# The second half of an embedding gate: seven block products for three pairs of K tiles, and low parts made by accumulating transfers

## The chip, the cores and the metric

The kernel runs on one core of one Trainium2 chip. Its time is the device time of one execution in microseconds, taken as the median of several runs. A profile of one execution gives the start and length of every instruction on the engines: TensorE (PE; its weight loads are PEld), VectorE (DVE), ScalarE (ACT), GpSimd (POOL) and SyncE (SP), whose queue issues most of the DMAs.

## What is computed

One layer of a decoder block on 256 tokens of width 2048, all in fp32. The change touches only the last step:

```
x = layer_norm(ALPHA * x + ffn, ln2_g, ln2_b)
x = x + jax.nn.sigmoid(x @ w_ple_gate) * (p @ w_ple_proj)   # w_ple_gate: 2048 x 2048
```

Before it come a combined input projection, gated linear attention and forgetting attention, their merge and output projection, a layer norm, a gated MLP with a causal convolution and another layer norm.

## The kernel before

**Weights in two parts.** TensorE multiplies in a rounded format. Each fp32 weight w is therefore split into hi, a rounded copy, and lo = w - hi, and activations likewise. A product of K tiles is three matmuls: hi by hi, hi by lo and lo by hi.

**Units.** All weights stream through the chip as 284 units, each of two K tiles (128 rows each) by 1024 columns, in two halves (one K tile each) of 512 KB. `prep()` (L207) makes a unit ready: for each half a load `raw` on SP's queue (L216), the rounded copy `hi` on ScalarE (`copy`, L112) and the subtraction `lo` on VectorE (L220). The tiles come from rings: 5 `raw`, 6 `hi`, 6 `lo`. A tile of a ring can be written again when the last reader of the tile six (five) places earlier is done. `unit()` prepares three units ahead. `prep_s()` (L167) makes a unit ready for seven products instead of eight: it takes four differences of weight blocks on VectorE (`differences`, L146) and splits the result into four hi and four lo pieces (b11 of 512 columns, b2, t13 and t24 of 1024). Each earlier stage that uses it has its list of pairs (`GV_S`, `WO_S`, `DN_S` and others); the gate has none.

**The gate.** It runs in two halves, pg0 (units 268 to 275, output columns 0 to 1023) and pg1 (units 276 to 283). `x_half` (L347) accumulates one half: four PSUM banks, one for each of two token tiles by two blocks of 512 columns; `x_mm` (L320) issues the matmuls, 24 of 512 columns per unit (2 K tiles, 2 token tiles, 3 products, 2 blocks). The units run one after the other, but the last two of pg1 (`tail=2`) run block by block, so that the first blocks are complete earlier. With `fine=True` (pg1 only) block (1,1) lies in two banks of 256 columns, `pg` and `pg_11b`, for all eight units; its matmuls there have 256 columns, twice as many.

**The end of a block.** `ev_o` (L1450 on) makes the output from a complete bank: tanh on ScalarE (L1459, `tho`), two VectorE operations (L1460 `tho`, L1462 `res`) that apply it to the projection of p (`ppk`) and add the layer's z, and a store on SP (L1464). pg0's four stores are held back and issued by `store_first` after pg1's first unit.

**Order.** The instructions of SP stay in written order. Those of the other engines are ordered ahead of time by a planner, and each engine's queue is in order: an instruction that waits holds back what stands behind it. POOL does little: some small operations, and DMAs of intermediate sums (`sd`, `td`) to DRAM in earlier stages.

Of the kernel before, what the change touches and what calls it, by code (L numbers as in the profile page):

```python
# [9 lines left out]
F32 = mybir.dt.float32  # L10
F32R = mybir.dt.float32r
BF16 = mybir.dt.bfloat16
U8 = mybir.dt.uint8
AF = mybir.ActivationFunctionType
ALU = mybir.AluOpType
# [4 lines left out]
P = 128  # L20
D = 2048
S = 256
# [26 lines left out]
OUT_ORDER = (tuple(range(8)), (0, 1, 3, 2, 5, 4, 6, 7))  # L49
# [3 lines left out]
WO_S = ((1, 3, 5), (1, 3, 5))  # L53
WO_C = (0, 2, 4, 6, 7)

DN_ORDER = (tuple(range(NF // 2)),
            (0, 1, 2, 3, 5, 4, 7, 9, 6, 11, 8, 13, 10, 15, 12, 17, 14, 16, 18, 19, 20, 21))
DN_S = ((1, 3, 5, 7, 9, 11, 13, 15, 17, 19), (1, 3, 5, 7, 9, 11, 13, 15, 17))


WO_T = ((3, 5), (1, 3, 5))
DN_T = ((3, 9, 15, 19), (5, 9, 13, 17))
AFF1 = ((0, 2, 3), (0, 2))
AFF2 = ((0, 2), (0, 2))
LN_ORDER = (1, 0, 3, 2)
# [7 lines left out]
def tile_block(ctx: ExitStack, tc: tile.TileContext, wu, wfv, wpp, xT_in, x_in, pT_in, wlr,  # L73
               chan, gnorm, lng, ident_in, mask_in, cmask_in, out):
    nc = tc.nc
# [26 lines left out]
    def t2(name):  # L102
        return sm.tile([P, 512], F32, tag="t2", bufs=6, name=name)
# [17 lines left out]
    for _ in range(8):  # L121
# [4 lines left out]
    NU = wu.shape[0]  # L126
    dn0 = NU - 16 - NF
    s_units = {b + nh * len(order[nh]) + i
               for b, order, sset in ((52, WO_ORDER, GV_S), (68, WO_ORDER, GR_S),
                                      (120, OUT_ORDER, WO_S), (dn0, DN_ORDER, DN_S))  # L130
               for nh in range(2) for i, n in enumerate(order[nh]) if n in sset[nh]}
    ready = {}

# [8 lines left out]
    def lo_tile(u, name):  # L142
        o = 0 if any(u in r for r in UA) else LO_SHIFT
        return rlo.tile([P, 1152], F32R, tag="lo", name=f"lo{name}")[:, o:o + 1024]
# [62 lines left out]
    def prep(pinned=False):  # L207
        u = n_prep[0]
        n_prep[0] += 1
        if u in s_units:  # L210
            prep_s(u)
            return
        his, los = [], []
        for h in range(2):
            raw = ring.tile([P, 1024], F32, tag="raw", bufs=5, name=f"raw{u}_{h}")
            nc.sync.dma_start(raw, wu[u, :, h * 1024:(h + 1) * 1024])  # L216
            hi = rhi.tile([P, 1024], F32R, tag="hi", name=f"hi{u}_{h}")
            copy(hi, raw)
            lo = lo_tile(u, f"{u}_{h}")
            i = nc.vector.tensor_tensor(lo, raw, hi.bitcast(F32), ALU.subtract)  # L220
            if pinned:
                tc.keep_in_program_order(i)
            his.append(hi)
            los.append(lo)
        ready[u] = (his, los)
# [212 lines left out]
    for u in range(8):  # L438
        hi, lo = fvu[u]
        for j in range(2):  # L440
            kt = 2 * u + j
            a = xT[kt // 4][:, kt % 4, :]
# [6 lines left out]
            for t, i, c in seq:  # L449
                o, n = fch[c]  # L450
                w, x = prods[t][i]
                nc.tensor.matmul(fbk[t][c][:, 0:n], lhsT=x, rhs=w[:, o:o + n],  # L452
                                 start=kt == 0 and i == 0, stop=kt == 15 and i == 2)
# [32 lines left out]
    for t in range(2):  # L486
        for c, (o, n) in enumerate(fch):
            n = min(n, 1024 - o)
# [279 lines left out]
        return o  # L768

    def s_half(nm, nh, order, sset, cl, st, zof, ev, tail=0, mid={}, end=None, ahead=3,  # L770
               residual=True):

        if nh == 0:
            C = [[mmtile(f"{nm}0_{t}{c}") for c in range(2)] for t in range(2)]
            p1, p5 = [mmtile(f"{nm}0_p{i}") for i in (1, 5)]
            p6, p7 = [mxtile(f"{nm}0_p{i}") for i in (6, 7)]
        else:  # L780
            C = [[f(f"{nm}1_{t}{c}") for c in range(2)] for t, f in enumerate((mxtile, mmtile))]
            p1, p5, p6, p7 = [mmtile(f"{nm}1_p{i}") for i in (1, 5, 6, 7)]
        prods = (p1, C[0][0], C[0][1], p5, p7, p6, C[1][0])
        left = (0, 1, 6, 3, 5, 4, 2)
        n, ns = len(order), len(sset)
        todo = {id(C[t][c]): 6 * (n - ns) for t in range(2) for c in range(2)}
        for p in prods:
            todo[id(p)] = todo.get(id(p), 0) + 3 * ns
        total = dict(todo)

        def mm(ps, x, w):
            nc.tensor.matmul(ps, lhsT=x, rhs=w, start=todo[id(ps)] == total[id(ps)],  # L792
                             stop=todo[id(ps)] == 1)
            todo[id(ps)] -= 1

        def classic(pair, w, toks=(0, 1), cs=(0, 1)):
            for j in range(2):
                for t in toks:
                    ah, al = cl(pair, j, t)
                    for x, v in ((ah, w[0][j]), (ah, w[1][j]), (al, w[0][j])):  # L800
                        for c in cs:
                            mm(C[t][c], x, v[:, c * 512:c * 512 + 512])

        def strassen(pair, ops):
            for ps, i, (hi, lo) in zip(prods, left, ops):
                ah, al = st(pair, i)
                for x, v in ((ah, hi), (ah, lo), (al, hi)):
                    mm(ps, x, v)

        def fold():  # L810
            g0, g1 = 2 * nh, 2 * nh + 1
            u = t2("fold")
            axpy = lambda z, p: nc.vector.scalar_tensor_tensor(z, z, ALPHA, p, ALU.mult, ALU.add)
            add = lambda z, p: nc.vector.tensor_tensor(z, z, p, ALU.add)
            if not residual:
                copy(zof(0, g0), p1)
                for o, x, p in ((u, zof(0, g0), p6), (zof(0, g1), u, p5), (zof(1, g0), u, p7),
                                (zof(1, g1), zof(1, g0), p5)):
                    nc.vector.tensor_tensor(o, x, p, ALU.add)
                return  # L820
            copy(u, p1)
            axpy(zof(0, g0), p1)
            add(u, p6)
            axpy(zof(0, g1), u)
            add(zof(0, g1), p5)
            add(u, p7)
            axpy(zof(1, g0), u)
            add(u, p5)
            axpy(zof(1, g1), u)

        for i, pair in enumerate(order[:n - tail]):
            (strassen if pair in sset else classic)(pair, unit())
            if i in mid:
                mid[i]()
            if pair in sset and not set(order[i + 1:]) & set(sset):
                fold()
        us = [unit(ahead) for _ in range(tail)]

        def tail_mm(t, c, i):
            classic(order[n - tail + i], us[i], (t,), (c,))  # L840
            if i == tail - 1:
                ev(t, c, C[t][c])

        if tail:
            end(tail_mm)
            return
        for t in range(2):
            for c in range(2):
                ev(t, c, C[t][c])
# [599 lines left out]
        for store in stores:  # L1449
            store()  # L1450

    for nh in range(2):
        def ev_o(t, c, ps, ab=(0, 512), nh=nh):
            th = t2("tho")
            r = t2("res")
            e = slice(*ab)
            w = slice(c * 512 + ab[0], c * 512 + ab[1])
            o = slice(nh * 1024 + w.start, nh * 1024 + w.stop)
            nc.scalar.activation(th[:, e], ps, AF.Tanh, bias=0.0, scale=0.5)  # L1459
            nc.vector.scalar_tensor_tensor(th[:, e], th[:, e], 1.0, pp[nh][:, t, w],  # L1460
                                           ALU.add, ALU.mult)
            nc.vector.scalar_tensor_tensor(r[:, e], th[:, e], 0.5, z2[nh][:, t, w],  # L1462
                                           ALU.mult, ALU.add)
            store = lambda: nc.sync.dma_start(out[t, :, o], r[:, e])  # L1464
            if nh == 0:
                stores.append(store)
            else:
                store()
        x_half(f"pg{nh}", x2T, 16, ev_o, pulls=2, begin=begin2 if nh == 0 else None,
               tail=2 if nh == 1 else 0, mid=((mid3, 4), (store_first, 0))[nh],  # L1470
               fine=nh == 1)
    assert n_used[0] == NU, (n_used[0], NU)


# [9 lines left out]
def _xst(w):  # L1484

    k, n = w.shape
    a = w.reshape(k // 256, 2, P, n // 1024, 1024).transpose(3, 0, 2, 1, 4)
    return a.reshape((k // 256) * (n // 1024), P, 2048)


def _sst(w, orders, ssets):


    out = []
    for nh, (order, sset) in enumerate(zip(orders, ssets)):
        for n in order:
            b = [[w[(2 * n + j) * P:(2 * n + j + 1) * P,
                    nh * 1024 + c * 512:nh * 1024 + c * 512 + 512] for c in range(2)]
                 for j in range(2)]
            out.append(np.concatenate([b[0][1], b[0][0], b[1][1], b[1][0]] if n in sset  # L1500
                                      else b[0] + b[1], 1))
    return np.stack(out)
# [11 lines left out]
def _layout(i):  # L1514
# [4 lines left out]
    for n in range(16):  # L1519
        br.append(bg[n:n + 1])  # L1520
        if n % 2 == 0:
# [6 lines left out]
         _sst(c("gv", 2048), WO_ORDER, GV_S), _sst(c("gr", 2048), WO_ORDER, GR_S), m[PSM1:]] + br  # L1528
        + [_sst(i["w_out"][0], OUT_ORDER, WO_S), gu,
           _sst(i["w_down"][0], DN_ORDER, DN_S),  # L1530
           _xst(i["w_ple_gate"][0])], 0)
    wfv = np.concatenate([c("fv", 1024), c("glr", 16), c("ff", 8)], 1)
    wfv = wfv.reshape(8, 2, P, NS).transpose(0, 2, 1, 3)
    x = _fold(i["x"][0])
# [40 lines left out]
```

## Time and profile before

| what | us |
|---|---|
| median of 3 runs | 1662.37 (1661.83 to 1663.08) |
| span of the profiled execution | 1661.1 |
| PE busy | 1655.3 |
| DVE busy | 1278.4 |
| ACT busy | 887.5 |
| POOL busy | 61.3 |
| DMA, mean | 231 GB/s |

The page gives no time of its own for the profiled execution beside its span; the median of the runs is 1.3 us above that span. The busy times are sums over the whole span. Times in the views count from the span's start; the gate's second half lies between some 1612 and 1657 us.

### The profile page before, as it was taken

How to read it: one execution, taken by the hardware profiler on the slowest of the kernel's cores; microseconds unless marked ns; L12 is line 12 of the kernel's file. 1: busy time of each engine (PE TensorE's matmuls, PEld its weight loads, DVE VectorE, ACT ScalarE, POOL GpSimd, SP SyncE). 2: the span in 40 equal slices, each digit the busy share in tenths (PEclk: the TensorE clock that was granted, in tenths of full speed). 3: DMA queues.
4: the chain of work that ended last, by engine and by line, in shares of the span. 5: the costliest groups of instructions: out<-in, count | busy, mean ns of one | idle time of the engine just before them, and what ended most of it. 6: DMA issues, size and time to landing. Idle time of an engine off the chain costs nothing.

```text
span 1661.1 us, 24309 instructions
## 1 busy us (share of the span) xinstructions
PE 1655.3 (100%) x8935; PEld 1438.3 (87%) x8935; DVE 1278.4 (77%) x1927; ACT 887.5 (53%) x1297; POOL 61.3 (4%) x204
## 2 busy tenths in 40 slices
PE   9999999999999999999999999999999999999999
PEld 9988888888888888888898888888888888888887
DVE  7666877888876757888987777877777787898774
ACT  6655555555554654455575455555555555556543
POOL 0100000000000000000010010000000000000000
PEclk9999999999999999999999999999999999999999
DMA  8745455546564557878856587777777668798554
GB/s 321 251 164 172 169 176 171 188 158 199 196 232 172 174 181 275 309 244 301 315 171 206 207 291 266 251 243 249 254 249 255 204 226 322 275 364 316 178 188 158
DMA packets 101959, 383.74 MB, mean 231 GB/s; under 512 B 11544, under 2 KB 12832, under 8 KB 95696
## 3 DMA queue, kind: packets, MB, share of 16 engines
q1 hardware_dynamic: 97584, 359.11, 62.1%
q0 software_dynamic: 4256, 23.08, 3.7%
q8 instruction: 70, 1.15, 0.3%
q14 instruction: 49, 0.40, 0.1%
HBM read 358.02 MB, written 24.13 MB: 230 GB/s over the span
## 4 chain that ended last, share of the span: by engine, by line
PE 98%; DMA 0%; DVE 0%; ACT 0%; POOL 0%; SPq 0%; issue 0%; POOLq 0%
PE dn L792 11%; PE psu L287 9%; PE psg L287 9%; PE psm L287 7%; PE pg L333 5%; PE psu L289 5%; PE psg L289 5%; PE gv L792 4%; PE wo L792 4%; PE psm L289 4%; PE psa L287 4%; PE dn_p L792 3%; PE gr L333 3%; PE fv L452 2%; PE gr L792 2%; PE psa L289 2%
## 5 line engine op out<-in xcount | busy, mean ns | idle before, releaser
L220 DVE TENSOR_TENSOR lo<-raw,hi 128x1024 fp32r<-128x1024 f32 x502 | 611.0, 1223 | 240.4 <-ACT hi L112 238.7
L112 ACT ACTIVATE hi<-raw 128x1024 fp32r<-128x1024 f32 x502 | 528.4, 1058 | 430.5 <-issue 169.2
L287 PE MATMUL psu<-x1T,hi 128*128 128x512 f32 x688 | 240.4, 392 | 0.0
L287 PE MATMUL psg<-x1T,hi 128*128 128x512 f32 x672 | 234.8, 392 | 0.0
L289 PE MATMUL psu<-x1T,lo 128*128 128x256 f32 x688 | 192.4, 280 | 0.0
L289 PE MATMUL psg<-x1T,lo 128*128 128x256 f32 x672 | 187.9, 280 | 0.0
L287 PE MATMUL psm<-xT,hi 128*128 128x512 f32 x512 | 181.2, 396 | 0.0
L287 PEld LDWEIGHTS psu<-x1T,hi 128*128 128x128 f32 x688 | 129.2, 188 | 27.6
L287 PEld LDWEIGHTS psg<-x1T,hi 128*128 128x128 f32 x672 | 126.2, 188 | 26.9
L289 PE MATMUL psm<-xT,lo 128*128 128x256 f32 x512 | 143.2, 280 | 0.0
L289 PEld LDWEIGHTS psu<-x1T,lo 128*128 128x128 f32 x688 | 130.7, 190 | 0.0
L289 PEld LDWEIGHTS psg<-x1T,lo 128*128 128x128 f32 x672 | 127.6, 190 | 0.0
L287 PEld LDWEIGHTS psm<-xT,hi 128*128 128x128 f32 x512 | 96.2, 188 | 19.7
L792 PE MATMUL dn<-hi,hC 128*128 128x512 f32 x400 | 111.3, 389 | 0.0
L289 PEld LDWEIGHTS psm<-xT,lo 128*128 128x128 f32 x512 | 97.2, 190 | 0.1
L287 PE MATMUL psa<-oT,hi 128*128 128x512 f32 x256 | 89.5, 392 | 0.0
L792 PEld LDWEIGHTS dn<-hi,hC 128*128 128x128 f32 x400 | 75.0, 188 | 15.6
L112 ACT ACTIVATE hi_t<-raw 128x1024 fp32r<-128x1024 f32 x40 | 42.5, 1063 | 66.0 <-DVE raw L148 51.5
L112 ACT ACTIVATE hi_b<-raw 128x512 fp32r<-128x512 f32 x66 | 55.4, 842 | 40.9 <-DMA raw<-in_wu_dram 15.2
L289 PE MATMUL psa<-oT,lo 128*128 128x256 f32 x256 | 71.6, 280 | 0.0
L194 DVE TENSOR_TENSOR lo_b<-raw,hi_b 128x512 fp32r<-128x512 f32 x66 | 62.5, 954 | 9.9 <-ACT hi_b L112 9.9
L333 PE MATMUL pg<-hi,x2T 128*128 128x512 f32 (+1 forms) x256 | 69.7, 380 | 0.0
(372 smaller groups left out, 3126.3 us busy)
## 6 DMA issues: line engine op xcount, KB each, us to landing
raw<-in_wu_dram SPq DMA_DIRECT2D x555, 512.0 KB, 4.9
td<-in_wu_dram SPq DMA_DIRECT2D x13, 1024.0 KB, 8.4
td<-td POOLq DMA_DIRECT2D x13, 1024.0 KB, 6.9
td<-td SPq DMA_DIRECT2D x13, 1024.0 KB, 7.5
hS<-sd SPq DMA_DIRECT2D x19, 512.0 KB, 7.6
fvraw<-in_wfv_dram SPq DMA_DIRECT2D x13, 524.0 KB, 6.9
sd<-hs POOLq DMA_DIRECT2D x20, 256.0 KB, 5.4
lnb<-in_lng_dram SPq DMA_DIRECT2D x4, 1024.0 KB, 9.8
```

Of the source, the lines that this page charges most:

```text
L112: return nc.scalar.activation(o, i, AF.Copy, bias=0.0, scale=scale)
L194: nc.vector.tensor_tensor(lo, src, hi.bitcast(F32), ALU.subtract)
L220: i = nc.vector.tensor_tensor(lo, raw, hi.bitcast(F32), ALU.subtract)
L287: nc.tensor.matmul(ps, lhsT=hi[i // 8 if hoff == 0 else 0][:, w0 % 1024:w0 % 1024 + P], rhs=a[:, kt % 4, :], start=first and i == 0, stop= ...
L289: nc.tensor.matmul(ps[:, 256:512], lhsT=lo[i // 8 if hoff == 0 else 0][:, w0 % 1024:w0 % 1024 + P], rhs=a[:, kt % 4, 0:256], start=False, ...
L333: nc.tensor.matmul(bs[j][:, 0:m], lhsT=x, rhs=v[:, o:o + m], start=first and i == 0, stop=last and i == 2)
L452: nc.tensor.matmul(fbk[t][c][:, 0:n], lhsT=x, rhs=w[:, o:o + n], start=kt == 0 and i == 0, stop=kt == 15 and i == 2)
L792: nc.tensor.matmul(ps, lhsT=x, rhs=w, start=todo[id(ps)] == total[id(ps)], stop=todo[id(ps)] == 1)
```

## The change

- Units 277, 279 and 281 (pairs 1, 3 and 5 of pg1) are prepared by `prep_s` and multiplied by `strassen` in `s_half`: seven block products, 21 matmuls of 512 columns. Four PSUM banks p1, p5, p6, p7 hold products that `fold` adds to `zg` in SBUF (one copy on ScalarE, four additions on VectorE); three of the products go straight to blocks. `g_sums` makes the sums of activation blocks that the products need, from `x2T`, on VectorE and ScalarE.
- pg1's other five units run in `s_half` as before, with 512 columns. Block (1,1) is cut in two halves of 256 columns only in the last two units.
- At a block's end `ev_g` first adds the bank to `zg` on VectorE; then `put` does what `ev_o` did. For pg0 nothing but the writing of it changes.
- For the second halves of units 270 to 276, 278 and 280 (`LO_DMA`) the low part comes in another way: ScalarE writes the negated rounded copy to `lo`, and POOL issues a DMA that adds the weights from DRAM to it.

The function `s_half`, as the changed kernel calls it (its core):

```
prods = (p1, C[0][0], C[0][1], p5, p7, p6, C[1][0])
left = (0, 1, 6, 3, 5, 4, 2)
def strassen(pair, ops):
    for ps, i, (hi, lo) in zip(prods, left, ops):
        ah, al = st(pair, i)
        for x, v in ((ah, hi), (ah, lo), (al, hi)):
            mm(ps, x, v)
...
for i, pair in enumerate(order[:n - tail]):
    (strassen if pair in sset else classic)(pair, unit())
    if i in mid:
        mid[i]()
    if pair in sset and not set(order[i + 1:]) & set(sset):
        fold()
```

`fold`, for `residual=False` (L826 to L829 of the changed kernel), is a copy and four additions. The diff:

```diff
--- before.py
+++ after.py
@@ -60,6 +60,9 @@
 
 WO_T = ((3, 5), (1, 3, 5))
 DN_T = ((3, 9, 15, 19), (5, 9, 13, 17))
+PG_ORDER = (tuple(range(8)), tuple(range(8)))
+PG_S = ((), (1, 3, 5))
+LO_DMA = tuple(range(270, 276)) + (276, 278, 280)
 AFF1 = ((0, 2, 3), (0, 2))
 AFF2 = ((0, 2), (0, 2))
 LN_ORDER = (1, 0, 3, 2)
@@ -127,7 +130,8 @@
     dn0 = NU - 16 - NF
     s_units = {b + nh * len(order[nh]) + i
                for b, order, sset in ((52, WO_ORDER, GV_S), (68, WO_ORDER, GR_S),
-                                      (120, OUT_ORDER, WO_S), (dn0, DN_ORDER, DN_S))
+                                      (120, OUT_ORDER, WO_S), (dn0, DN_ORDER, DN_S),
+                                      (NU - 16, PG_ORDER, PG_S))
                for nh in range(2) for i, n in enumerate(order[nh]) if n in sset[nh]}
     ready = {}
 
@@ -217,6 +221,12 @@
             hi = rhi.tile([P, 1024], F32R, tag="hi", name=f"hi{u}_{h}")
             copy(hi, raw)
             lo = lo_tile(u, f"{u}_{h}")
+            if h == 1 and u in LO_DMA:
+                copy(lo, raw, -1.0)
+                nc.gpsimd.dma_start(lo, wu[u, :, 1024:2048], accum_op=ALU.add)
+                his.append(hi)
+                los.append(lo)
+                continue
             i = nc.vector.tensor_tensor(lo, raw, hi.bitcast(F32), ALU.subtract)
             if pinned:
                 tc.keep_in_program_order(i)
@@ -768,7 +778,7 @@
         return o
 
     def s_half(nm, nh, order, sset, cl, st, zof, ev, tail=0, mid={}, end=None, ahead=3,
-               residual=True):
+               residual=True, fine=False):
 
 
 
@@ -788,8 +798,8 @@
             todo[id(p)] = todo.get(id(p), 0) + 3 * ns
         total = dict(todo)
 
-        def mm(ps, x, w):
-            nc.tensor.matmul(ps, lhsT=x, rhs=w, start=todo[id(ps)] == total[id(ps)],
+        def mm(ps, x, w, e=slice(0, 512)):
+            nc.tensor.matmul(ps[:, e], lhsT=x, rhs=w, start=todo[id(ps)] == total[id(ps)],
                              stop=todo[id(ps)] == 1)
             todo[id(ps)] -= 1
 
@@ -841,6 +851,21 @@
             if i == tail - 1:
                 ev(t, c, C[t][c])
 
+        if fine:
+            for t, c in ((0, 0), (0, 1), (1, 0)):
+                for i in range(tail):
+                    tail_mm(t, c, i)
+            half = mmtile(f"{nm}{nh}_11b")[:, 0:256]
+            last = [(x, v[:, 512:1024]) for i in range(tail) for j in range(2)
+                    for ah, al in (cl(order[n - tail + i], j, 1),)
+                    for x, v in ((ah, us[i][0][j]), (ah, us[i][1][j]), (al, us[i][0][j]))]
+            for x, v in last:
+                mm(C[1][1], x, v[:, 0:256], slice(0, 256))
+            for k, (x, v) in enumerate(last):
+                nc.tensor.matmul(half, lhsT=x, rhs=v[:, 256:512], start=k == 0,
+                                 stop=k == len(last) - 1)
+            ev(1, 1, C[1][1], half)
+            return
         if tail:
             end(tail_mm)
             return
@@ -1449,26 +1474,60 @@
         for store in stores:
             store()
 
-    for nh in range(2):
-        def ev_o(t, c, ps, ab=(0, 512), nh=nh):
-            th = t2("tho")
-            r = t2("res")
-            e = slice(*ab)
-            w = slice(c * 512 + ab[0], c * 512 + ab[1])
-            o = slice(nh * 1024 + w.start, nh * 1024 + w.stop)
-            nc.scalar.activation(th[:, e], ps, AF.Tanh, bias=0.0, scale=0.5)
-            nc.vector.scalar_tensor_tensor(th[:, e], th[:, e], 1.0, pp[nh][:, t, w],
-                                           ALU.add, ALU.mult)
-            nc.vector.scalar_tensor_tensor(r[:, e], th[:, e], 0.5, z2[nh][:, t, w],
-                                           ALU.mult, ALU.add)
-            store = lambda: nc.sync.dma_start(out[t, :, o], r[:, e])
-            if nh == 0:
-                stores.append(store)
-            else:
-                store()
-        x_half(f"pg{nh}", x2T, 16, ev_o, pulls=2, begin=begin2 if nh == 0 else None,
-               tail=2 if nh == 1 else 0, mid=((mid3, 4), (store_first, 0))[nh],
-               fine=nh == 1)
+    def put(z, nh, t, c, ab=(0, 512)):
+        th = t2("tho")
+        r = t2("res")
+        e = slice(*ab)
+        w = slice(c * 512 + ab[0], c * 512 + ab[1])
+        o = slice(nh * 1024 + w.start, nh * 1024 + w.stop)
+        nc.scalar.activation(th[:, e], z, AF.Tanh, bias=0.0, scale=0.5)
+        nc.vector.scalar_tensor_tensor(th[:, e], th[:, e], 1.0, pp[nh][:, t, w],
+                                       ALU.add, ALU.mult)
+        nc.vector.scalar_tensor_tensor(r[:, e], th[:, e], 0.5, z2[nh][:, t, w],
+                                       ALU.mult, ALU.add)
+        return lambda: nc.sync.dma_start(out[t, :, o], r[:, e])
+
+    x_half("pg0", x2T, 16, lambda t, c, ps: stores.append(put(ps, 0, t, c)), pulls=2,
+           begin=begin2, mid=(mid3, 4))
+
+    def g_cl(pair, j, t):
+        kt = 2 * pair + j
+        a = x2T[kt // 4][:, kt % 4, :]
+        return a[:, t * P:t * P + P], a[:, 256 + t * P:256 + t * P + P]
+
+    gS_ = {}
+
+    def g_sums():
+        for i, pair in enumerate(PG_S[1]):
+            o = s8([P, 4, 256], F32R, name=f"gS{pair}")
+            a = x2T[pair // 2][:, pair % 2 * 2:pair % 2 * 2 + 2, :].bitcast(F32)
+            y = t2("gy").rearrange("p (k t) -> p k t", t=S)
+            nc.vector.tensor_tensor(y, a[:, :, 0:256], a[:, :, 256:512], ALU.add)
+            v = s_sums(y)
+            copy(o[:, :, 0:P], v)
+            nc.vector.tensor_tensor(o[:, :, P:256], v, o[:, :, 0:P].bitcast(F32), ALU.subtract)
+            gS_[pair] = o
+
+    def g_st(pair, i):
+        if i < 3:
+            return g_cl(pair, (0, 1, 1)[i], (0, 0, 1)[i])
+        return cell(gS_[pair], i - 3)
+
+    zg = s8([P, 2, 2, 512], name="zg")
+
+    def ev_g(t, c, ps, half=None):
+        z = zg[:, t, c, :]
+        es = (slice(0, 512),) if half is None else (slice(0, 256), slice(256, 512))
+        for e in es:
+            nc.vector.tensor_tensor(z[:, e], z[:, e], ps[:, e], ALU.add)
+        for e in es:
+            if e.start:
+                nc.vector.tensor_tensor(z[:, e], z[:, e], half, ALU.add)
+            put(z[:, e], 1, t, c, (e.start, e.stop))()
+
+    g_sums()
+    s_half("pg", 1, PG_ORDER[1], PG_S[1], g_cl, g_st, lambda t, g: zg[:, t, g - 2, :], ev_g,
+           2, {0: store_first}, residual=False, fine=True)
     assert n_used[0] == NU, (n_used[0], NU)
 
 
@@ -1528,7 +1587,7 @@
          _sst(c("gv", 2048), WO_ORDER, GV_S), _sst(c("gr", 2048), WO_ORDER, GR_S), m[PSM1:]] + br
         + [_sst(i["w_out"][0], OUT_ORDER, WO_S), gu,
            _sst(i["w_down"][0], DN_ORDER, DN_S),
-           _xst(i["w_ple_gate"][0])], 0)
+           _sst(i["w_ple_gate"][0], PG_ORDER, PG_S)], 0)
     wfv = np.concatenate([c("fv", 1024), c("glr", 16), c("ff", 8)], 1)
     wfv = wfv.reshape(8, 2, P, NS).transpose(0, 2, 1, 3)
     x = _fold(i["x"][0])
```

## The prediction

> **What bounds the kernel now.** I read the page's busy times first, then the chain of waits, then the stretch that the change touches by windows and by groups of matmuls, and last the DMAs.
>
> ```profile
> span 1661.1 us, 24309 instructions
> PE 1655.3 (100%) x8935; PEld 1438.3 (87%) x8935; DVE 1278.4 (77%) x1927; ACT 887.5 (53%) x1297; POOL 61.3 (4%) x204
> PEclk9999999999999999999999999999999999999999
> PE 98%; DMA 0%; DVE 0%; ACT 0%; POOL 0%; SPq 0%; issue 0%; POOLq 0%
> raw<-in_wu_dram SPq DMA_DIRECT2D x555, 512.0 KB, 4.9
> ```
>
> TensorE is busy for the whole span at full clock, and 98% of the chain is TensorE. The median of the runs, 1662.4 us, is 1.3 above the span; I carry a difference of spans over to it. So a matmul taken away is worth its time, but only while what feeds TensorE is early. No other engine shows in the chain, and a list of what TensorE waits for between 1559 and 1657 us is empty: the feeds' slack has to be worked out.
>
> ```profile
> 1577.00:1587.00 10.00, 10.00 (x51) 8.23 (x51) 8.39 (x10) 5.28 (x7) 0.00 (x0) 1.00 0.90 313
> 1612.00:1657.00 45.00, 45.00 (x242) 38.43 (x240) 23.50 (x27) 15.31 (x18) 0.00 (x0) 1.00 0.44 152
> ```
>
> These windows list PE, PEld, DVE, ACT, POOL, then clock, DMA share and GB/s. In the gate's second half (1612 to 1657) VectorE is busy for half of the time, and that half's feeds look easy. Around 1580, where the first half starts, the DMA engines are 90% busy.
>
> **The matmuls.** The second half's groups and the chain give the price:
>
> ```profile
> L333 PE MATMUL pg<-hi,x2T 128*128 128x512 f32 x96 | 30.1, 393 | 0.0
> L333 PE MATMUL pg<-lo,x2T 128*128 128x512 f32 x48 | 16.9, 393 | 0.0
> L333 PE MATMUL pg<-hi,x2T 128*128 128x256 f32 x32 | 8.4, 283 | 0.0
> L333 PE MATMUL pg_11b<-hi,x2T 128*128 128x256 f32 x32 | 8.3, 280 | 0.0
> L333 PE MATMUL pg_11b<-lo,x2T 128*128 128x256 f32 x16 | 4.5, 283 | 0.0
> L333 PE MATMUL pg<-lo,x2T 128*128 128x256 f32 x16 | 4.5, 281 | 0.0
> ...
> 1526.04 33.32 PE dn L792 x147
> 1611.67 1.07 PE L333 MATMUL pg<-hi,x2T 128*128 128x512 f32 x4
> ...
> L333 PE MATMUL pg_11b<-hi,x2T x32: 274/281/285, 1613.7 to 1656.7; 128*128 128x256 f32 x32
> ```
>
> 144 matmuls of 512 columns and 96 of 256. One of 512 takes 33.32/147 = 0.2267 us in a row (393 ns is its length in the pipe). The third of the four matmuls that start at 1611.67 is the half's first: 1612.13. The last half starts at 1656.7 (last row), so the half ends near 1656.8, and its 96 matmuls of 256 columns share 44.7 − 144 × 0.2267 = 12.1 us, or 0.126 each. The change gives three units 21 products instead of 24, and halves the last block in two units only: 171 of 512 and 24 of 256, 38.77 + 3.02 = 41.8 us. TensorE saves **2.9 us**: nine products for 2.04, and 36 rejoined pairs at 2 × 0.126 − 0.227 for 0.9. That is the most it can bring, 0.17%. About 0.2% (3.3 us) is what a measurement of this kernel can tell from no change; a gain beyond it has no source here.
>
> **The end.** The chain after the matmuls, in order of time (start, length):
>
> ```profile
> 1654.17 0.61 ACT tho L1459
> 1654.80 0.70 DVE tho L1460
> ...
> 1657.04 0.39 ACT tho L1459
> 1657.45 0.44 DVE tho L1460
> 1657.91 0.42 DVE res L1462
> ```
>
> From the third block's end (1654.15) to the last result (1658.33) it is 4.2 us now, of which 2.9 is TensorE's last block. The changed end adds `zg` on VectorE ahead of every tanh: one add of 0.69 for the third block and three of 256 columns for the last. In the written order VectorE runs add, tho, add(a), res, add(b), tho(a), add(half), res(a), tho(b), res(b). The third block's tho cannot start before 0.03 + 0.69 + 0.03 + 0.61 = 1.4 after that block's end, so the queue of one tho and one res of 512 (some 0.65 each) and seven steps of 256 starts there. A step of 256 is 0.42 alone and, I estimate, 0.37 where the next one overlaps it: 1.4 + 1.3 + 2.6 = 5.3 (5.6 without overlap). Hence **+1.1 us**. Its lower bound is 0.45, one add and its hop behind the last matmul; the upper one 1.5.
>
> The folds of four adds (L829 of the new file) wait for products that end two tail blocks earlier, and VectorE's half-empty window covers them. The sums of x2T (`g_sums`: on VectorE six instructions of 512 columns at 0.69 and twelve of 128 at an estimated 0.25, 7 us; three copies of 0.6 on ScalarE) fall at about 1620, where VectorE idles:
>
> ```profile
> 1617.94 0.69 DVE L1462 SCALAR_TENSOR_TENSOR res<-tho,z 128x512 f32<-128x512 f32 x1
> 1624.23 1.23 DVE L220 TENSOR_TENSOR lo<-raw,hi 128x1024 fp32r<-128x1024 f32 x1 [5.59 <-ACT hi L112]
> ...
> 1623.14 1.06 ACT L112 ACTIVATE hi<-raw 128x1024 fp32r<-128x1024 f32 x1 [8.30 <-DMA raw<-in_wu_dram]
> 1625.27 1.06 ACT L112 ACTIVATE hi<-raw 128x1024 fp32r<-128x1024 f32 x1 [1.07 <-DMA raw<-in_wu_dram]
> ```
>
> If that cover were gone they would cost up to 7. Without any new stall the change is −2.9 + 1.1 = **−1.8 us**.
>
> **The accumulating transfers.** Nine second halves get their low part from ScalarE (a negated copy, 1.06) and then a transfer that POOL issues and that adds 512 KB of weights to it; before, VectorE did it in one 1.23 us subtraction. Nine subtractions less are worth nothing in themselves, since VectorE is not in the chain, and nine copies more lie in ScalarE's idle time (53% busy, and 8.30 us idle ahead of 1623.14). What counts is when the low part is there. Let L be the time from that issue to landing. The trace has no accumulating transfer. Its nearest rows:
>
> ```profile
> L216 SPq DMA_DIRECT2D raw<-in_wu_dram x5: 327/328/328, 1591.0 to 1601.1; - x5
> ...
> DMA to landing us min/median/max: 3.5/3.8/5.0
> ...
> L1464 SPq DMA_DIRECT2D out_dram<-res x9: 332/333/344, 1613.3 to 1658.4; - x9
> ...
> DMA to landing us min/median/max: 1.9/2.2/2.5
> ...
> L1320 POOL DMA_DIRECT2D sd<-hs x20: 539/539/547, 895.3 to 1295.2; - x20
> ...
> DMA to landing us min/median/max: 3.8/5.4/10.8
> ...
> L164 POOL DMA_DIRECT2D td<-td x13: 531/537/581, 640.4 to 1275.3; - x13
> ...
> DMA to landing us min/median/max: 5.1/6.9/12.7
> ```
>
> A plain 512 KB load on SP's queue takes 3.5 to 5.0 when little else runs. 256 KB takes 2.2 from SP and 5.4 from POOL, at best 1.9 and 3.8: POOL's path adds 1.9 to 3.2. So a plain 512 KB from POOL would be some 5.4 to 7.0. Adding needs the old value read as well as the new one, 1024 KB read in all; the row with POOL's issue and that size is `td`, 6.9 (5.1 to 12.7). I take **L = 6.9**, with 4.0 as the low end (the two reads cost nothing, and POOL little) and 10 as the high one.
>
> The Trainium skill, "Collectives: The Full Stack", Part 3, "The bandwidth ceiling", says that an add in the DMA is slow because it needs two source reads, and gives a measured ratio of 1.93 to a copy. No run here shows that yet; by it the load's streaming part doubles, which would put L near the `td` row, as I have it.
>
> Now the three places where L is not covered, by counting in the changed order. Counts run at 0.2267.
>
> Unit 278. Its low slot (ring of six) was unit 276's second one, last read by the half's 22nd product, which ends near 1617.3; the copy ends at 1618.4 and POOL issues. The first product that reads it is the 44th: 1612.13 + 43 × 0.2267 = 1621.9. Stall: L − 3.5, 3.4 at L = 6.9. VectorE would have needed 1.2, and no stall. TensorE's queue is in order, so everything behind it slips.
>
> Unit 280. SP issues four deferred stores ahead of unit 279's loads, and in the new order unit 277's and 278's low parts stand between the results that they store, so those loads land some 1.3 later than the 1625.25 seen above: 1626.5. Then one copy (1.06), one subtraction (1.22), three differences (2.0), the t24 copy (1.06) and unit 280's three copies (3.2): POOL issues near 1635.1. The 110th product reads it at 1612.13 + 109 × 0.2267 = 1636.8, plus the slip. Moreover unit 279's b2 piece waits for unit 277's slot, whose last reader (the 54th product, 1624.5) stands behind the stalled one: beyond a slip of 2.0 the whole preparation is pushed too. So the stall is L − 1.7 − 3.4 + (3.4 − 2.0) = 3.2 at 6.9; together the two are L − 1.7 for L up to 5.5 and 2L − 7.2 beyond.
>
> Unit 270, in the busy DMA stretch:
>
> ```profile
> 1571.27 1.08 ACT L112 ACTIVATE hi<-raw 128x1024 fp32r<-128x1024 f32 x1
> ...
> 1579.32 0.62 PE L333 MATMUL pg<-lo,x2T 128*128 128x512 f32 x2
> ```
>
> The negated copy follows the first row, so the issue is at 1573.2, and the second row's matmuls need it: slack 6.2, stall 0.7 at L = 6.9. Units 271 to 276 follow at 5.4 us a unit, with copies further ahead; hidden up to about L = 8. The six transfers move 3 MB more at 1573 to 1610, 10 us of the 313 GB/s above; the raw loads, fetched five buffers ahead, take it without a stall by the count.
>
> Sum: −1.8 + 3.4 + 3.2 + 0.7 = +5.5; I take off 0.5 because a stall at 270 also lets the later preparation catch up. **+5.0 us: 1667.4.**
>
> **The rivals.** (A) The forecast: late accumulating transfers. At L = 6.0 it is −1.8 + 4.8 = +3.0, so the measurable loss begins just above 6; at 8 it is −1.8 + 8.8 + 1.8 = +8.8. For it speaks the POOL row of 5.4 for half the bytes; against it, that such rows stand beside other traffic.
>
> (B) The transfer is as quick as a plain one, 4.0 to 6: the stalls are 2.3 to 4.8 and the change is +0.5 to +3.0, within 0.2%. The minima of the `sd` and `td` rows speak for it. The Trainium skill, "DMA: Bandwidth & Descriptors", "Anatomy of one DMA — SWDGE (gpsimd) path", gives 2.0 us plus the bytes over 436 GB/s, an estimate of 3.2 us for 512 KB; with that the change would end near −0.3. The medians of the POOL rows disagree with it, 5.4 for 256 KB where it gives 2.6.
>
> (C) No stall at all: −1.8, 1660.6, still no measurable gain. It needs L under 2, below every row.
>
> (D) The adds stream at a third of the rate or queue behind raw loads, L of 10: stalls 12.8 and 3.8, so +14.8; and units 271, 273 and 274 begin to wait. It decides from L = 9. The `sd` maximum, 10.8, speaks for it; that it is one of twenty, against. That the transfers are dropped or moved by the scheduler is excluded: POOL's order gains nine of them.
>
> **How the numbers follow.** A 0.54, B 0.32, C 0.04, D 0.10. A loses its lowest edge to "same"; faster gets 0.02 for an unseen gain. Faster 0.02, same 0.35, slower 0.63. The range takes in B from L = 4 (+0.5, 1662.9; I put 1662.5) and reaches into D up to +13.6 (1676). A's own range is +3 to +9.
>
> **What would show it.** Right: waits of TensorE on DMA at L802 for `lo`, about 3 us each, twice; POOL rows at L226 landing in about 7; PE busy 2.9 lower; last block to last result 5.3. Wrong: those rows land under 5 and TensorE waits less than 2 in all (B), or waits at pg0 as well (D), or waits for DVE or ACT at unit 279 (a chain that I placed too early).

## The result, and the profile after

The changed kernel takes 1680.6 us (1678.66 to 1680.91, 4 runs), the kernel before 1662.26: **18.3 us slower**, a ratio of 1.0108 [1.0096, 1.012]. The forecast was 1667.4 with a range up to 1676. The direction was right, the size was not. The profiled execution is the fastest of the four, 1678.66 with a span of 1676.3, so its trace accounts for the 15.2 us between the two profiled spans.

From the page of the changed kernel:

```profile
span 1676.3 us, 24305 instructions
PE 1656.0 (99%) x8890; PEld 1436.6 (86%) x8890; DVE 1292.7 (77%) x1964; ACT 902.8 (54%) x1316; POOL 69.0 (4%) x213
...
PE 97%; DMA 2%; issue 1%; DVE 0%; ACT 0%; POOL 0%; POOLq 0%
```

TensorE has 45 instructions fewer and is yet 0.7 us longer busy, and it idles. The list of what TensorE waits for from 1559 us on, empty before, has three rows (total, times, longest):

```profile
PE pg L802 <- DMA lo<-in_wu_dram: 8.9, 2, 6.1
PE pg L343 <- DMA lo<-in_wu_dram: 3.8, 1, 3.8
PE pg_p L802 <- ACT hi_t L115: 0.7, 1, 0.7
```

The places are those of the prediction: unit 270 (3.8), unit 278 (2.8), unit 280 (6.1). The chain, in order of time, names the transfers with their length from issue, and below it the tile view gives L over all nine:

```profile
1572.87 9.52 DMA lo<-in_wu_dram
...
1623.53 6.07 DMA lo<-in_wu_dram
...
1642.73 9.64 DMA lo<-in_wu_dram
...
1668.15 0.70 DVE zg L1522
...
1673.11 0.42 DVE res L1486
...
L226 POOL DMA_DIRECT2D lo<-in_wu_dram x9: 863/872/937, 1572.9 to 1642.7; - x9
...
DMA to landing us min/median/max: 6.1/8.6/10.1
```

What the prediction has no term for is in the windows behind the waits (PE, PEld, DVE, ACT, POOL, clock, DMA share, GB/s):

```profile
1579.00:1583.00 4.00, 0.57 (x2) 0.48 (x3) 0.29 (x1) 0.93 (x1) 0.88 (x1) 1.00 1.07 301
1583.00:1585.00 2.00, 2.00 (x9) 1.67 (x8) 0.00 (x0) 0.60 (x1) 0.00 (x0) 0.66 1.03 266
1585.00:1587.00 2.00, 2.00 (x6) 1.60 (x5) 1.29 (x2) 0.05 (x1) 0.00 (x0) 0.50 1.08 287
...
1630.00:1634.00 4.00, 4.00 (x19) 3.32 (x18) 1.67 (x4) 1.43 (x3) 0.00 (x0) 1.00 1.01 364
...
1652.00:1655.00 3.00, 2.59 (x6) 2.11 (x7) 0.25 (x1) 0.00 (x0) 0.00 (x0) 0.50 0.19 78
```

At unit 270 the granted clock falls to 0.50 behind the wait, for 3.4 us (1583.6 to 1587.0); at unit 280 it falls during the wait already and stays there for 6.8 us (1648.5 to 1655.3), of which TensorE works 2.9. Behind the wait at unit 278 (1630 to 1634) it stays at 1.00. At half clock matmuls start 0.427 us apart instead of 0.227, which costs 1.8 and 1.5 us. That is also why TensorE's busy time did not fall.

The account: waits 13.4, half clock 3.3, end +1.2 (the last result comes 5.4 us after the third block, 4.2 before), TensorE's work −2.9: +15.0 of 15.2.

### The profile page after: what moved, and what is told of

It reads as the page before. It is cut to its first block, busy times and chain, and to the rows that moved or that the text cites. A ratio compares the mean times of both kernels' runs of the same rounds, so it can differ in the third digit from the quotient of the medians.

```text
span 1676.3 us, 24305 instructions
## 1 busy us (share of the span) xinstructions
PE 1656.0 (99%) x8890; PEld 1436.6 (86%) x8890; DVE 1292.7 (77%) x1964; ACT 902.8 (54%) x1316; POOL 69.0 (4%) x213
## 4 chain that ended last, share of the span: by engine, by line
PE 97%; DMA 2%; issue 1%; DVE 0%; ACT 0%; POOL 0%; POOLq 0%
PE dn L802 10%; PE psu L297 9%; PE psg L297 9%; PE psm L297 7%; PE psu L299 5%; PE psg L299 5%; PE gv L802 4%; PE wo L802 4%; PE psm L299 4%; PE psa L297 4%; PE dn_p L802 3%; PE fv L462 3%; PE gr L343 3%; PE pg L343 2%; PE gr L802 2%; PE psa L299 2%
## 5 line engine op out<-in xcount | busy, mean ns | idle before, releaser
L230 DVE TENSOR_TENSOR lo<-raw,hi 128x1024 fp32r<-128x1024 f32 x487 | 592.1, 1222 | 230.8 <-ACT hi L115 229.8
L115 ACT ACTIVATE hi<-raw 128x1024 fp32r<-128x1024 f32 x496 | 521.8, 1057 | 410.7 <-issue 169.1
L115 ACT ACTIVATE hi_t<-raw 128x1024 fp32r<-128x1024 f32 x46 | 48.9, 1062 | 72.9 <-DVE raw L152 52.8
L115 ACT ACTIVATE hi_b<-raw 128x512 fp32r<-128x512 f32 x72 | 60.4, 842 | 49.2 <-DMA raw<-in_wu_dram 22.4
L198 DVE TENSOR_TENSOR lo_b<-raw,hi_b 128x512 fp32r<-128x512 f32 x72 | 68.1, 954 | 19.7 <-ACT hi_b L115 19.6
L198 DVE TENSOR_TENSOR lo_t<-raw,hi_t 128x1024 fp32r<-128x1024 f32 x46 | 56.3, 1223 | 9.7 <-ACT hi_t L115 8.4
```

Of the source, the lines that this page charges most:

```text
L115: return nc.scalar.activation(o, i, AF.Copy, bias=0.0, scale=scale)
L198: nc.vector.tensor_tensor(lo, src, hi.bitcast(F32), ALU.subtract)
```

## The experiments

Each time is compared with the kernel before on the same chip (median 1662.2 to 1662.3).

**No accumulating transfer.**

```diff
-LO_DMA = tuple(range(270, 276)) + (276, 278, 280)
+LO_DMA = ()
```

> No accumulating transfer: all nine low parts come from VectorE's subtraction again; the seven products, the fold and the new end stay. Theory (the transfers land late, and all of the loss hangs on them): TensorE's waits on lo at units 270, 278 and 280 go, and so does the half clock behind two of them; 2.9 us less TensorE work against 1.1 more at the end leave 1660.4, up to 1662 if unit 279's t24 piece is late by itself (0.7 us in the changed kernel). Rival (the loss is the preparation of the seven-product units, four differences and four copies in a row behind late loads): TensorE still waits at units 279 to 281, 1667 or more.

Measured: 1664.65, a ratio of 1.0015 [1.0006, 1.0024]. 15.9 of the 18.3 us hang on the transfers, but 2.4 remain where the theory had a gain of 1.8. What TensorE waits for, and VectorE's window over the second half:

```profile
PE pg_p L802 <- ACT hi_t L115: 1.3, 2, 0.7
PE pg L802 <- DVE lo_b L198: 0.5, 1, 0.5
PE pg L802 <- ACT gS L115: 0.5, 1, 0.5
PE pg L802 <- DVE lo L230: 0.3, 1, 0.3
...
1611.60:1655.00 43.40, 40.69 (x174) 31.68 (x173) 41.06 (x61) 21.38 (x26) 0.00 (x0) 1.00 0.43 146
```

2.6 us of idle time in five waits. They cost more than that: from its first matmul to its last the half takes 46.0 us, 4.5 more than the 41.5 of a kernel with the same products and no wait (its rows stand under "Why the prediction was wrong"). The two matmuls next to a wait are further apart too. VectorE is busy for 41.1 of 43.4 us; before it was 23.5 of 45. So the seven products have a price of their own, which my theory lacked, though smaller than the rival's 1667.

**The same transfers without the add.**

```diff
-                nc.gpsimd.dma_start(lo, wu[u, :, 1024:2048], accum_op=ALU.add)
+                nc.gpsimd.dma_start(lo, wu[u, :, 1024:2048].bitcast(F32R))
```

> The nine transfers stay on POOL's queue with the same waits but copy the weights over lo instead of adding them (so lo holds the weights themselves: the subtraction is left out). Theory (the add doubles the transfer's work in the DMA engines, and that work is shared with the raw loads): issue to landing falls from a median of 8.6 us to 5 to 6.5, TensorE's waits from 12.7 us to 3 to 6 without a half clock, 1664 to 1667. Rival (POOL's queue itself is slow, whatever the transfer does): landing stays above 8 and the time near 1680.

This kernel leaves the subtraction out: `lo` holds the weights themselves. Measured: 1675.84, 1.0083 [1.0069, 1.0097], between the two and nearer to the rival. The DMA view from 1560 us on, first of the changed kernel, then of this one (packets, MB, share of 16 engines; median to landing):

```profile
q0 software_dynamic: 1296, 4.72, 21.6%
...
lo<-in_wu_dram POOLq DMA_DIRECT2D x9, 512.0 KB, 8.6
```

```profile
q0 software_dynamic: 1296, 4.72, 12.3%
...
lo<-in_wu_dram POOLq DMA_DIRECT2D x9, 512.0 KB, 7.2
...
DMA to landing us min/median/max: 5.4/7.2/7.9
...
1621.96 6.54 DMA lo<-in_wu_dram
...
1581.00:1582.50 1.50, 1.50 (x9) 1.28 (x9) 0.00 (x0) 0.00 (x0) 0.00 (x0) 0.88 1.02 360
1582.50:1585.00 2.50, 2.50 (x8) 2.02 (x7) 1.29 (x2) 0.60 (x1) 0.00 (x0) 0.50 1.07 388
```

The add takes 1.76 times the DMA engines' time for the same bytes, but only 1.4 of the 8.6 us to landing. A plain copy from POOL is already too late here. Its wait at unit 270 was 2.1 us, and the clock fell to 0.50 behind it, as it did behind the other two (3.2 and 4.0 us). How much of the 7.2 us is POOL's queue and how much SP's loads beside it, no run separates.

**Only the two late transfers, and only the seven early ones.** In the first, `LO_DMA = (278, 280)`:

> Accumulating transfers for units 278 and 280 only; units 270 to 276 go back to VectorE. Theory (each late transfer costs its own stall): the 3.8 us at unit 270 and the half clock behind it (1.7) go; 2.8 at unit 278 and about 6 at unit 280 with its half clock (1.7) stay, 1669 to 1672. Rival (the seven transfers before them crowd the DMA engines and make the late two late): both shrink to under 2 us each, 1663 to 1665.

Measured: 1674.32, 1.0072 [1.0058, 1.0086]. In the second, `LO_DMA = tuple(range(270, 277))`:

> Accumulating transfers for units 270 to 276 only; units 278 and 280 go back to VectorE. Theory (each late transfer costs its own stall): 3.8 us at unit 270 and 1.7 of half clock stay and the rest goes, -1.8 + 5.5 = +3.7, 1666. Rival (the first half hides its transfers but for a knock-on that shows later): 1671 or more with waits at 279 to 281; if unit 270's wait costs nothing, 1660.5.

Measured: 1670.96, 1.0056 [1.0043, 1.0068]. Their waits on transfers:

```profile
PE pg L802 <- DMA lo<-in_wu_dram: 9.5, 2, 6.6
...
1624.00:1628.00 4.00, 4.00 (x11) 3.17 (x12) 1.49 (x3) 1.18 (x3) 0.00 (x0) 0.57 1.02 353
```

```profile
PE pg L343 <- DMA lo<-in_wu_dram: 4.3, 1, 4.3
```

Against the kernel without transfers (+2.4) the late two cost 9.7 (net of the five short waits, which that trace no longer has) and the early seven 6.3; 2.4 + 9.7 + 6.3 = 18.4, the whole. The parts add up; the early transfers do not make the late ones late. Both times lie above what the theory gave (1669 to 1672, and 1666), since it started from −1.8. The second is near the rival's 1671, but not for the rival's reason: its other waits are the same five, of 2.6 us, as without any transfer. With the first kernel the clock fell behind unit 278's wait too (0.57 in the window of 1624 to 1628), which in the profiled execution of the changed kernel it did not.

**Units 272 to 276 only, and unit 270 only.**

> The changed kernel with accumulating transfers for units 272 to 276 only. Theory (a transfer costs time only where its landing is later than TensorE's need; 272 to 276 have over 10 us between issue and need): no wait on lo, and the time of the kernel without any such transfer, 1664.6. Rival (their traffic delays raw loads of units 277 to 279, or the move of five subtractions off VectorE helps): 1666 or more, or 1663 or less.

Measured: 1664.33, 1.0012 [1.0003, 1.0021]: the time without any transfer. They took 8.8 to 10.2 us to land, but five transfers with time in hand cost and bring nothing.

> The changed kernel with one accumulating transfer, that of unit 270. With its siblings of units 271 and 272 in flight it took 9.5 us to land, the one of unit 278 with little beside it 6.1. Theory S (the siblings crowd it): it lands in 7 or less, TensorE waits under 1 us there, 1664.5 to 1665.5. Theory R (SP's raw loads, queued ahead, crowd it): 8.5 or more, a wait of 3 or more and a half clock after it, 1668 to 1671.

Measured: 1670.79, 1.0054 [1.0041, 1.0068]: this one transfer is the whole of the early part (8.6 against 8.7 over the kernel before). It took 10.8 us without any sibling:

```profile
PE pg L343 <- DMA lo<-in_wu_dram: 5.1, 1, 5.1
...
DMA to landing us min/median/max: 10.8/10.8/10.8
...
1574.00:1576.00 2.00, 2.00 (x11) 1.65 (x10) 1.47 (x3) 2.00 (x3) 0.00 (x0) 1.00 0.84 211
1576.00:1578.00 2.00, 2.00 (x10) 1.68 (x9) 2.00 (x3) 1.18 (x3) 0.00 (x0) 1.00 0.98 260
1578.00:1580.00 2.00, 0.64 (x3) 0.19 (x1) 1.80 (x2) 0.98 (x1) 0.00 (x0) 1.00 1.00 203
```

The DMA engines are full meanwhile (share 0.84, then 0.98 to 1.00). So the sibling transfers do not make it late; the crowding with SP's loads is what is left (theory R), though no run takes the loads away to show it.

**Where the remaining 2.4 us are.** Three kernels without transfers: the four stores put later, so that SP issues unit 279's loads first; the activation sums made in the first half (with the call that runs it moved below their definition, and `mid3`, two loads on SP's queue, one unit later); both.

```diff
-    s_half("pg", 1, ..., 2, {0: store_first}, residual=False, fine=True)
+    s_half("pg", 1, ..., 2, {1: store_first}, residual=False, fine=True)
...
-           begin=begin2, mid=(mid3, 4))
+           begin=begin2, mid=(lambda: (mid3(), g_sums()), 5))
```

> The kernel without accumulating transfers, with the four deferred stores of the first half put behind unit 277's products instead of unit 276's, so that SP issues unit 279's loads ahead of them. Theory X (unit 279's loads are late because SP's queue stands behind stores that wait for VectorE): the waits at unit 279 go, 1660.5 to 1661.5. Theory Y (VectorE's queue is full: 41.1 of 43.4 us busy in the second half, with the activation sums ahead of unit 279's pieces): the loads land some 8 us earlier and the waits stay, 1664.5. Theory Z (both, one behind the other): 1664 to 1665 here.

> The kernel without accumulating transfers, with the activation sums made during the first half (7 us of VectorE moved from 1620 to some 1600 us). Theory X: unit 279 waits for its loads as before and only the wait for the sums (0.5 us idle, 0.9 with its refill) goes, 1663.5 to 1664.5. Theory Y: the waits go, 1660.5 to 1661.5. Theory Z: 1663.5 to 1664.5.

> Both moves. X and Y: no better than the better of the two alone. Z: only here do TensorE's waits go; 2.9 us less TensorE work against 1.2 more at the end, 1660.5 to 1661.2, faster than the kernel before by 0.1%.

Measured: stores later 1664.37 (1.0015 [1.0006, 1.0024]); sums earlier 1667.1 (1.0029 [1.0018, 1.004]), worse than any theory had it; both 1662.63 (1.0001 [0.9993, 1.001]). With the sums earlier the longest wait is one of 1.6 us:

```profile
PE pg L802 <- ACT hi_b L115: 1.6, 1, 1.6
```

Behind it the granted clock was 0.50 from 1631.4 to 1634.8, which costs up to 1.7 us; no theory had that. Neither move alone removes the waits (2.1 us with the stores later, 2.4 with the sums earlier), both together remove all but one of 0.3 us by the start times of the matmuls: theory Z for the waits. But the time did not come to 1661. The windows of the second half and the end of the chain with both moves:

```profile
1611.40:1656.00 44.60, 42.11 (x196) 34.81 (x194) 40.19 (x52) 20.94 (x26) 0.00 (x0) 1.00 0.40 142
...
1655.80 0.34 DVE zg L1525
...
1657.07 0.42 DVE res L1486
```

TensorE is done 2.5 us earlier in its half than before, and VectorE, in a row without a gap of over 0.7 us from 1640 on (four low parts, the fold, the blocks), ends 4.1 us after the last matmul instead of 1.6. The wait of TensorE became VectorE's queue.

**Less work for VectorE.** With both moves, block (1,1) is added to `zg` ahead of its tail and its two halves have a bank each. Once with transfers for units 274 to 276, once without and with seven products for pairs 1 and 3 only (`PG_S = ((), (1, 3))`).

```diff
             half = mmtile(f"{nm}{nh}_11b")[:, 0:256]
+            ev(1, 1, C[1][1], None, True)
...
-            for x, v in last:
-                mm(C[1][1], x, v[:, 0:256], slice(0, 256))
+            half0 = mmtile(f"{nm}{nh}_11a")[:, 0:256]
+            for k, (x, v) in enumerate(last):
+                nc.tensor.matmul(half0, lhsT=x, rhs=v[:, 0:256], start=k == 0,
+                                 stop=k == len(last) - 1)
...
-            ev(1, 1, C[1][1], half)
+            ev(1, 1, half0, half)
```

> The kernel with both moves and with less VectorE work near the end: block (1,1) outside the last two units is added to zg before its tail runs, its two halves have a bank each (one 256-column add less in the last queue), and units 274 to 276 have accumulating transfers, which land early enough. Theory V (with TensorE's waits gone, VectorE's queue of the fold and the last blocks sets the end: last result 4.1 us after the last matmul, 1.6 in the kernel before): 1660.5 to 1661.5, last result some 3 us after the last matmul. Rival (the row of dependent steps at the end takes its time whatever stands ahead): 4.1 stays, 1662.5.

> As the kernel with both moves and the early add, no accumulating transfer, but seven products for pairs 1 and 3 only, so that the fold comes a unit and a half earlier and VectorE has some 7 us less to do. TensorE saves 2.2 instead of 2.9. Theory V: no wait of TensorE, last result 2.3 to 2.8 after the last matmul, 2.2 - 1.0 = 1.2 less, 1661.0 to 1661.6. Rival (every pair is worth its three matmuls and VectorE has room): worse than the three pairs by 0.7.

Measured: 1661.94 (0.9997 [0.9989, 1.0006]), last result 3.5 us after the last matmul, between theory V and its rival; and **1660.72** (0.9991 [0.9982, 1.0]), 2.5 after, a little under theory V's 1661.0 to 1661.6. TensorE waits for nothing in either. The windows of the second half:

```profile
1611.40:1656.00 44.60, 41.69 (x196) 34.83 (x194) 40.03 (x53) 21.28 (x26) 0.00 (x0) 1.00 0.45 148
```

```profile
1611.40:1656.00 44.60, 42.23 (x198) 35.29 (x196) 35.83 (x47) 19.93 (x24) 0.00 (x0) 1.00 0.44 150
```

Two pairs beat three, although TensorE works 0.7 us longer: with 4 us less VectorE work the queue at the end is shorter. The two kernels differ in the three transfers as well; those of units 272 to 276 changed nothing above, so I put the 1.2 us down to the pairs, but no run has three pairs without transfers and with the early add. It is the fastest version here, 1.5 us under the kernel before, at the edge of what can be told from no change.

**The joined halves alone.** No seven products; block (1,1) whole until its last two units.

> No seven-product pair and no accumulating transfer: only block (1,1) is kept whole until its last two units, where its halves go to two banks that are added to a copy of the rest. 36 rejoined matmuls are worth 0.9 us by the prediction, one add behind the last matmul costs 0.45: 1661.8. If halves cost TensorE nothing beyond their columns: 1662.7.

Measured: 1662.03 (0.9998 [0.9989, 1.0007]), too near to tell by its time. The trace tells: no wait, and from the half's first matmul to its last 43.55 us where it was 44.6, a saving of 1.0; the last result 2.5 instead of 1.6 after that, a loss of 0.9. The add behind the last matmul was put too low (0.45).

## Why the prediction was wrong

The forecast was +5.0, the trace's account is +15.0. Of the 10.0 between them, TensorE's waits are 6.6 (13.4 against the 3.4 + 3.2 + 0.7 − 0.5 = 6.8 of the sum), the half clock 3.3 and the end 0.1.

**TensorE's work, −2.9: right.** In the kernel with three pairs, the early add and no wait, the half runs from its first matmul (1611.29) to its last (1652.8):

```profile
1611.29 0.62 PE L802 MATMUL pg<-hi,x2T 128*128 128x512 f32 x2
...
L868 PE MATMUL pg_11b<-hi,x2T x8: 279/283/283, 1651.5 to 1652.8; 128*128 128x256 f32 x8
```

41.5 us, against 44.6 before: −3.1. **The end, +1.1: right** (5.4 us from the third block, 5.3 forecast).

**The three places: right.** For unit 278 the count gave a wait of L − 3.5; with L = 6.07 that is 2.6, measured 2.8.

**L = 6.9: the term that failed.** It was 9.5 at unit 270, 6.1 at 278 and 9.6 at 280. I took one number for all three, from a row of earlier stages, and put down the maxima (10.8, 12.7) as rare. Eight of the nine transfers took 7.7 to 10.1, at a DMA share of 0.9 to 1 (the transfers themselves included); and I had the share of 0.90 on the table when I gave unit 270 the same L as unit 278. The 6.1 of unit 278 is that of a transfer that was issued while the DMA engines were idle (share 0.00 from 1623 to 1624); the loads that filled them came 2 us behind it. Doubling the read was not the heart of it: the plain copy needed 7.2. The 0.5 that I took off for catching up is shown by no run. The Trainium skill, "Collectives: The Full Stack", Part 3, gives 1.93 for an add against a copy, there for ReduceScatter against AllGather; the 1.76 times of DMA time above agrees in kind. The formula of its page "DMA: Bandwidth & Descriptors", "Anatomy of one DMA — SWDGE (gpsimd) path", an estimate of 3.2 us here, holds for no transfer of this size on POOL's queue here: the fastest plain one took 5.4.

**Unit 280's issue: put 2.0 too early.** It came 25.8 us after the half's start (1642.73 − 1616.9); the count gave 23.0 and a push of 0.8. Unit 278's transfer shared the DMA engines with unit 279's first two loads: they landed 6.8 and 7.4 us after their issue (7.0 and 7.5 in the kernel with the late two), and 3.8 to 5.9 in the four kernels with no transfer at unit 278. So an extra transfer costs twice, by its own landing and by the loads that it delays. But not all of the 2.0 is its doing: without any transfer the stores hold these loads about 1 us longer, and the second one lands 16.2 us after the half's start, here 16.8, where the count had 14.4.

**Half clock: no term.** 3.3 us in the trace. The median lies 3 us further from the kernel before than the profiled spans do; a half clock behind unit 278 too, as in the kernel with the late two, would give half of that. The record has the mean granted clock of the other three executions, 0.995 to 0.996 against 0.997 in the profiled one: some 3 to 7 us more at half clock, an estimate from these rounded figures. Behind which waits they came stays open. The Trainium skill, "TensorE: Matmul & The Clock Gate", Part 1, names an idle window of about 3.4 us; here waits of 1.6 and 2.1 us were followed by a half clock and one of 2.8 was not.

**The covers: never added up.** I set the sums, the fold and the pieces of unit 279 against VectorE's idle half, each by itself. Together they fill it: 23.5 us of 45 became 41.1 of 43.4. The "no new stall" case of −1.8 did not exist for this order of instructions; without transfers it is +2.4.

Rival D (an L of 10, +14.8) is the nearest to what happened; it had a chance of 0.10, its price lacked the clock and VectorE's waits, and units 271, 273 and 274 did not wait as it had them.

## What to carry to other kernels

A latency is read from rows of the same load: the transfer issued where the DMA engines were 90% busy took 9.5 to 10.8 us, near the maximum of the nearest row (10.8) and not its median (5.4). Such a transfer is harmless only where its need lies further off than that (units 272 to 276 cost nothing). When a change puts several pieces of work "beside" TensorE, add them up for the engine that takes them, and price a wait of TensorE of 1.6 us or more with the half-clock time that can follow it. Fewer block products with less side work (two pairs) seem to beat more of them here.

## What the runs showed of the hardware

- With waits of 1.6 to 6.6 us TensorE's granted clock fell to 0.50: up to 1.4 us after work had resumed, or, in the waits of 5.1, 6.1 and 6.6 us, before that. It stayed there for 3.4 us, in the last two for 6.8 (1.5 and 1.8 us lost in the changed kernel). With one of 2.8 us it stayed at 1.00.
- An accumulating DMA took 1.76 times the DMA engines' time of a plain one; issued with the DMA engines idle, at unit 278, it landed as early (6.1 us, the plain one 6.5).
- POOL was held 0.87 us by the issue of an accumulating DMA, 0.53 by that of the plain one in its place.
- Short waits of TensorE cost more than their idle time: with five of them, 2.6 us in all, the half took 4.5 us longer than without.
